# First attention head's loads placed behind the gate blocks, two buffers for the scans' gates, one buffer ring for the scans' level copies

## The chip, the core and the metric

The kernel runs on one core of a Trainium2 chip. The metric is the device time of one execution in microseconds (us). Before the change the median of three runs is 3580.6 us (3577.68 to 3582.16). The engines are named as in the profile: PE is TensorE (PEld its weight loads), DVE is VectorE, ACT is ScalarE, POOL is GpSimd, SP is SyncE, which here only issues DMAs. Each engine takes its instructions in order, and so does each queue of DMA issues.

## What is computed

Two layers of a hybrid encoder on x of 2048 tokens by 1024 features. One input projection of 4128 columns feeds three groups of heads: four heads of gated linear attention and four of HGRN2, both as two-way scans in chunks, and four heads of differential softmax attention. Each group's output is normalised and multiplied by its own SiLU gate; one output projection, a norm and the residual end the layer.

```python
for layer in range(DEPTH):
    h = rms_norm(x, norm_pre[layer])
    proj = h @ w_in[layer]
    (gq, gk, gv, gg, gaf, gab, dq, dk, dv, dg, hq, hzf, hzb, hi, hg) = jnp.split(proj, offs, axis=-1)
    y_a = gla_branch(gq, gk, gv, gg, gaf, gab, ...)      # two scans, forward and backward
    y_b = diff_branch(dq, dk, dv, dg, ...)               # softmax(q1 k1) - lam * softmax(q2 k2), times v
    y_c = hgrn_branch(hq, hzf, hzb, hi, hg, ...)         # two scans
    y = jnp.concatenate([y_a, y_b, y_c], axis=-1) @ w_out[layer]
    x = x + rms_norm(y, norm_post[layer])
```

## The kernel before

**Stages of a layer.** The tokens are cut into two halves ("parts" 0 and 1), the input projection into 18 blocks of columns (lists `first` and `rest`). The loop at the end of the stage `s1` first runs all blocks for part 0, then all for part 1, and during part 1 the scans. Then come attention (`Unit`, with the scans' state products `Inter` between) and the output projection. In layer 0 part 1 with the scans lies at about 405 to 986 us of the span, attention at 986 to 1600 us; in layer 1 at about 2172 to 2765 us and 2765 to 3380 us.

**The blocks of part 1.** Blocks 9 and 10 are the attention values, 11 and 12 its keys, 13 and 14 its queries (`do_qk`), 15 to 17 gates (`do_gate`). A block of part 1 gets its weights `whi`, `wlo` (1 MB each) again from `dr_w` on POOL's DMA queue (line 226, two buffers). A block of `do_qk` makes products in PSUM (line 330), which DVE (lines 369, 371), POOL (372, 375) and ACT (374) turn into `u` and `rh`; both are stored to `dr_q` or `dr_k` by SP (377, 378). A block of `do_gate` makes its products at line 339; DVE copies them to `z` (428), ACT and DVE make the sigmoid in `lsm` (354, 430), POOL multiplies by the norm weight `nw` (432) and by `lsm` (433), SP stores to `dr_gate` (434). `nw` has one buffer and is loaded by SP (412). All these row tiles (`u`, `rz`, `rh`, `z`, `lse`, `lsm`) share one ring of six buffers (`EVB`), and a tile that is stored keeps its buffer until its store has landed. The products of part 1 have four PSUM banks.

**The scans.** There are 12 groups: 3 kinds (`ti`: one of the linear attention, two of HGRN2) for each of 4 stretches of 512 tokens. `scan_group` is a generator of 8 steps; a group starts 5 steps behind the last one (`LAG`), and `SCHED` says how far the scans have been written out behind each block. A group loads `qr`, `kt` and its decay gates `gt` (SP; lines 546 and 550). `gt` has one buffer (`GTB`); it is read by line 560, and as the totals of level 1 by lines 649, 651 and 657. The levels 3 to 7 multiply masked copies of `kt` and `qt`: ACT makes `qp`, `kp` for the linear attention in a ring of six buffers (`QMB`, tag `qm`), `kc`, `qc` for HGRN2 in one of four (`KCB`, tag `kc`), and PE multiplies them (600, 619). `qt` has two buffers and is stored to `dr_qs` by SP (683) at the end. The diagonal goes by PE transposes (671) and DVE sums `dg` (672), products with the values (692) and states (714, stored to `dr_u` at 733) end a group.

**The first head's loads.** When block 14 has been written out, the scans' buffers are given back and the pool `ak` takes their place. `load_q` loads the queries of three pairs of 128-query blocks (24 DMAs of 64 KB on SP, line 774), `head_keys(0)`, behind block 15, the keys (4 DMAs of 512 KB, on POOL's queue for the first head, line 754), `head_values(0)`, behind block 16, the values (1 MB on POOL's queue, line 761).

**What sets the order.** Up to the end of the projection a scheduler decides each engine's order, with a timeline of its own, from the order in which the code is written, the priorities and the buffers. In attention the order is written out by hand.

Of the kernel before, what the change touches and what calls it, by code (L numbers as in the profile page):

```python
# [11 lines left out]
F32 = mybir.dt.float32  # L12
# [9 lines left out]
P = 128  # L22
# [7 lines left out]
KC = D // P  # L30
EVB = 6
EPB = 4
KCB = 4
PRB = 4
ATB = 3
QMB = 6
OIB = 1
QSB = 3
QRB = 1
GTB = 1  # L40
VB = 1
TTB = 1
SCHED = [2, 4, 6, 6, 6, 6, 6, 6, 6, 9, 12, 12, 12, 12, 12, 12, 12, 12]
# [18 lines left out]
def tile_hybrid_encoder(  # L62
# [9 lines left out]
    nc = tc.nc  # L72
# [219 lines left out]
    for l in range(DEPTH):  # L292
# [15 lines left out]
        with ExitStack() as s1:  # L308
# [71 lines left out]
            def t2_rows(ap, t2):  # L380
                return ap[256 * t2:256 * t2 + 256, :].rearrange("(j p) c -> p j c", p=P)
# [19 lines left out]
                        nc.sync.dma_start(dr_vr[t0:t0 + 1024, i].rearrange("(c p) n -> c p n", p=P),  # L401
                                          bass.AP(odd.tensor, odd.offset + (P - 1) * 512, [(P * 512, 8), (-512, P), (1, 64)]))

            low = {}

            def do_gate(c0, d0, part):
                w = wload(c0, 288 if d0 == 0 else 256, part)
                nw = ev.tile([P, 256], F32, tag="nw", name="nw", bufs=1)
                src = {0: gla_norm, 768: hgrn_norm}.get(d0, diff_norm)
                n = src.shape[-1]  # L410
                for i in range(0, 256, n):
                    nc.sync.dma_start(nw[:, i:i + n], src[l:l + 1].to_broadcast([P, n]))
                if src is diff_norm:
                    nc.vector.tensor_scalar(nw, nw, 1.0 - lam_init, None, op0=ALU.mult)
                for t2 in range(4 * part, 4 * part + 4):
                    z = ev.tile([P, 512], F32, tag="t", name="z")
                    if d0 == 0:
                        if t2 % 2 == 0:
                            low[t2 // 2] = ev.tile([P, 4, 32], F32, tag="low", name="low", bufs=2)
                        for j in range(2):  # L420
                            t = 2 * t2 + j
                            ps = acc([P, 288], "pp", part)
                            mm_rows(ps, w, t, 288)
                            nc.vector.tensor_copy(z[:, 256 * j:256 * j + 256], ps[:, :256])
                            nc.scalar.copy(low[t2 // 2][:, t % 4], ps[:, 256:])
                    else:
                        ps = mm_time(w, t2)
                        nc.vector.tensor_copy(z, ps.rearrange("p j c -> p (j c)"))
                    _, m = log_sig(z)
                    nc.scalar.activation(m, m, AF.Exp)  # L430
                    zn = z.rearrange("p (j c) -> p j c", j=2)
                    nc.gpsimd.tensor_tensor(zn, zn, nw.unsqueeze(1).to_broadcast([P, 2, 256]), op=ALU.mult)
                    nc.gpsimd.tensor_tensor(z, z, m, op=ALU.mult)
                    nc.sync.dma_start(t2_rows(dr_gate, t2)[:, :, d0:d0 + 256], zn)

            def do_ch(c0, dst, scale, part):
                w = wload(c0, 256, part)
# [92 lines left out]
            sc = sc_st.enter_context(tc.tile_pool(name=f"sc{l}", bufs=1, side="left"))  # L530

            def scan_group(ti, g, tot):
# [18 lines left out]
                v = sc.tile([P, 4, ncol], F32, tag="v", name="v", bufs=VB)  # L551
# [27 lines left out]
                def gla_level(h, m2):  # L579
                    arr = [(2 * h, m2), (h, 2), (1, h)]  # L580
                    pms = []
                    for b in range(2):
# [4 lines left out]
                        back = [(P, 2), (-2 * h, 64 // h), (-1, h)]  # L587
                        qp = sc.tile([P, 2, 256], F32, tag="qm", name="qp", bufs=QMB)
                        for i in range(2):
# [16 lines left out]
                def hgrn_level(h, n2):  # L606

                    m = n2
                    arr = [(2 * h, m), (h, 2), (1, h)]
                    kc = sc.tile([P, 512], F32, tag="kc", name="kc", bufs=KCB)  # L610
                    nc.scalar.copy(custom(kc, 0, arr), custom(kt, 0, [(2 * h, m), (512 + h, 2), (1, h)]))
                    qc = sc.tile([P, 512], F32, tag="kc", name="qc", bufs=KCB)
                    nc.scalar.copy(custom(qc, 0, arr), custom(qt, 512, [(2 * h, m), (h - 512, 2), (1, h)]))
                    pm = [one_bank([P, 4, P], "pm") for _ in range(2)]
                    for c in range(4):
                        cs = slice(c * P, (c + 1) * P)
                        for hd in range(2):
                            rows = slice(64 * hd, 64 * hd + 64)
                            nc.tensor.matmul(pm[hd][:, c], kc[rows, cs], qc[rows, cs], start=True, stop=True)  # L619
                    return [(atp[0][:, hd], pm[hd], 0) for hd in range(2)]  # L620
# [3 lines left out]
                for lev in range(1, 8):  # L624
                    if lev > 2:
                        yield
                    h = 1 << (lev - 1)
# [119 lines left out]

            kv, qs_of, ga_of = {}, {}, [None]

            def head_keys(h):  # L750
                k = ak.tile([P, 2, L], F32R, tag="ks", name="ks", bufs=2)
                r = slice(64 * (h % 2), 64 * (h % 2) + 64)
                for p0 in range(0, P, 32):
                    (nc.sync if h else nc.gpsimd).dma_start(
                        k[p0:p0 + 32].bitcast(F32), dr_k[h // 2, p0 // 64, p0 // 32 % 2, r].rearrange("(c p) t -> p c t", p=32))
                ks = [k[:, 0], k[:, 1]]
                kv[h] = [ks, None]

            def head_values(h):
                v = ak.tile([P, NT, P], F32, tag="vt", name="vt", bufs=2)  # L760
                nc.gpsimd.dma_start(v, dr_v[:, h * P:(h + 1) * P].rearrange("(c p) n -> p c n", p=P))
                kv[h][1] = v

# [4 lines left out]
            def load_q(h, qp):  # L768
                qh = ak.tile([P, 2, 256], F32R, tag="aqh", name="aqh", bufs=3)
                ql = ak.tile([P, 2, 256], F32R, tag="aql", name="aql", bufs=3)  # L770
                r = slice(64 * (h % 2), 64 * (h % 2) + 64)
                for i, q in enumerate((qh, ql)):
                    for p0 in range(0, P, 32):
                        nc.sync.dma_start(q[p0:p0 + 32].bitcast(F32), dr_q[h // 2, p0 // 64, i, r, qp * 256:(qp + 1) * 256]
                                          .rearrange("(c p) t -> p c t", p=32))
                qs_of[h, qp] = qh, ql
# [8 lines left out]
            for i, b in enumerate(first + rest):  # L785
                b(1)
                scans(LAG * SCHED[i] if i < SC_END else len(work))
                if i == SC_END:
                    sc_st.close()
                    psum_close("m")  # L790
                    psum_open("t", f"pst{l}", "right")
                    at_st = ExitStack()
                    ak = at_st.enter_context(tc.tile_pool(name=f"ak{l}", bufs=1, side="left"))
                    for qp in range(3):
                        load_q(0, qp)
                if i == SC_END + 1:
                    head_keys(0)
                if i == SC_END + 2:
                    head_values(0)
            w_in_st.close()  # L800
            psum_close("s")
            psum_open("b", f"psb{l}", "left")
# [387 lines left out]
```

## Time and profile before

| | |
|---|---|
| median of the runs | 3580.6 us |
| the profiled execution | 3580.0 us, span 3578.0 us |
| PE busy | 3491.2 us, 98% of the span |
| DVE, ACT, POOL busy | 65%, 57%, 36% |
| granted clock of PE, mean | 0.988 |
| DMA | 544.59 MB, mean 152 GB/s |

The profile's busy time of PE counts matmuls whose ends are modelled, so a busy PE is not a PE at its best. Stretches are read by window: the busy time of each engine, the granted clock (1.00 is 2.4 GHz, 0.50 is 1.2 GHz), and the share of time in which the DMA engines were busy.

### The profile page before, as it was taken

To read this page: it belongs to the slowest core of one execution; us is meant where nothing else is said; L and a number is where in the kernel's file an instruction comes from. 1 tells how busy PE (TensorE), PEld (TensorE's weight loads), DVE (VectorE), ACT (ScalarE), POOL (GpSimd) and SP (SyncE) were. 2 spreads that over 40 slices of the span, in tenths; PEclk is the share of its full clock that TensorE was granted. 3 is DMA by queue.
4 is the path that set the end of the run, shared out by engine and by line. 5 is a ranking of instruction groups with operands and counts; after the bars stand their busy time and mean duration, and the time that the engine had idled before them with its cause. 6 is when DMAs were issued, how large, how long until landed. Compare 5 with 4: busy or idle time off the path is not lost.

```text
span 3578.0 us, 62684 instructions
## 1 busy us (share of the span) xinstructions
PE 3491.2 (98%) x23296; PEld 3151.1 (88%) x23296; DVE 2331.3 (65%) x4164; ACT 2046.3 (57%) x4692; POOL 1280.7 (36%) x1302
## 2 busy tenths in 40 slices
PE   7999999999899999999999999999998999999999
PEld 7898988988889999998898999889888889999887
DVE  5333578775299988985324336777843998989733
ACT  4531457653378888874226225576524888888722
POOL 4237310013466655610032472000134765656100
PEclk9999999999999999999999999999999999999999
DMA  6667545545653353214356665555465423433143
GB/s 238 214 230 241 202 151 172 164 145 179 184 140 75 108 137 100 89 50 156 121 205 232 221 228 180 172 163 167 134 190 167 129 73 116 132 93 101 35 135 118
DMA packets 323120, 544.59 MB, mean 152 GB/s; under 512 B 49088, under 2 KB 208512, under 8 KB 304128
## 3 DMA queue, kind: packets, MB, share of 16 engines
q1 hardware_dynamic: 300032, 426.54, 37.8%
q0 software_dynamic: 20672, 111.94, 9.8%
q8 instruction: 185, 3.03, 0.4%
q10 hardware_dynamic: 2112, 2.10, 0.2%
q14 instruction: 119, 0.97, 0.1%
HBM read 313.83 MB, written 228.59 MB: 152 GB/s over the span
## 4 chain that ended last, share of the span: by engine, by line
PE 75%; DVE 13%; DMA 5%; ACT 4%; issue 1%; SPq 1%; POOL 0%; DVEq 0%; ACTq 0%; POOLq 0%
PE pp L339 15%; PE pp L330 15%; PE po L991 10%; PE pob L1100 9%; PE s L928 5%; PE s L929 5%; PE pt L980 5%; DVE mx L933 4%; PE pm L619 2%; DVE e L974 2%; PE po L692 2%; PE pu L714 1%; PE poi L875 1%; DMA dr_q<-rh 1%; DMA gt<-dr_gg 1%
## 5 line engine op out<-in xcount | busy, mean ns | idle before, releaser
L933 DVE TENSOR_REDUCE mx<-s 128x1 f32<-128x1024 f32 x512 | 623.2, 1218 | 59.5 <-PE s L929 58.0
L339 PE MATMUL pp<-whi,hhi 128*128 128x256 f32 (+1 forms) x2048 | 591.5, 289 | 19.9 <-issue 14.2
L942 ACT ACTIVATE e<-s,mx 128x1024 f32<-128x1024 f32 x512 | 572.7, 1123 | 30.1 <-DVE mx L933 12.0
L339 PE MATMUL pp<-wlo,hhi 128*128 128x256 f32 (+1 forms) x2048 | 588.9, 288 | 0.0
L339 PE MATMUL pp<-whi,hlo 128*128 128x256 f32 (+1 forms) x2048 | 587.7, 287 | 0.4 <-DVE hlo L198 0.4
L991 PEld LDWEIGHTS po<-vt,wt 128*128 128x128 f32 x4096 | 534.3, 191 | 46.0 <-ACT o L998 3.5
L991 PE MATMUL po<-vt,wt 128*128 128x128 f32 x4096 | 540.1, 275 | 1.6 <-ACT o L998 1.6
L928 PE MATMUL s<-ks,aqh 128*128 128x512 f32 x1024 | 449.8, 439 | 12.9 <-ACT e L942 11.2
L339 PEld LDWEIGHTS pp<-whi,hhi 128*128 128x128 f32 x2048 | 393.8, 192 | 23.1 <-issue 21.7
L330 PE MATMUL pp<-hhi,whi 128*128 128x512 f32 x1024 | 407.7, 398 | 0.0
L330 PE MATMUL pp<-hlo,whi 128*128 128x512 f32 x1024 | 406.7, 397 | 0.0
L330 PE MATMUL pp<-hhi,wlo 128*128 128x512 f32 x1024 | 404.5, 395 | 0.0
L929 PE MATMUL s<-ks,aql 128*128 128x512 f32 x1024 | 403.4, 394 | 0.0
L339 PEld LDWEIGHTS pp<-whi,hlo 128*128 128x128 f32 x2048 | 394.2, 193 | 1.8 <-DVE hlo L198 0.8
L339 PEld LDWEIGHTS pp<-wlo,hhi 128*128 128x128 f32 x2048 | 393.4, 192 | 1.6 <-issue 0.2
L984 ACT COPY wt<-pt 128x512 f32<-128x512 f32 x512 | 301.3, 588 | 152.3 <-PE pt L980 149.2
L974 DVE SCALAR_TENSOR_TENSOR e<-e,gam 128x1024 f32<-128x1024 f32 x256 | 350.0, 1368 | 0.0
L980 PE MATMUL pt<-ident,e 128*128 128x128 f32 x2048 | 307.8, 273 | 0.4 <-ACT wt L984 0.3
L226 POOL DMA_DIRECT2D whi<-dr_w x32 | 17.6, 550 | 667.5 <-PE pp L339 341.7
L980 PEld LDWEIGHTS pt<-ident,e 128*128 128x128 f32 x2048 | 239.9, 141 | 1.8 <-ACT wt L984 1.0
L928 PEld LDWEIGHTS s<-ks,aqh 128*128 128x128 f32 x1024 | 194.9, 190 | 42.5 <-ACT e L942 18.2
L330 PEld LDWEIGHTS pp<-hhi,whi 128*128 128x128 f32 x1024 | 192.7, 188 | 43.5 <-issue 0.2
(184 smaller groups left out, 6846.2 us busy)
## 6 DMA issues: line engine op xcount, KB each, us to landing
dr_w<-whi SPq DMA_DIRECT2D x30, 1024.0 KB, 3.9
dr_w<-wlo SPq DMA_DIRECT2D x30, 1024.0 KB, 4.9
whi<-dr_w POOLq DMA_DIRECT2D x30, 1024.0 KB, 5.5
wlo<-dr_w POOLq DMA_DIRECT2D x30, 1024.0 KB, 8.6
wraw<-in_w_in_dram POOLq DMA_DIRECT2D x56, 512.0 KB, 6.3
dr_gate<-z SPq DMA_DIRECT2D x64, 256.0 KB, 2.4
aqh<-dr_q SPq DMA_DIRECT2D x256, 64.0 KB, 2.1
aql<-dr_q SPq DMA_DIRECT2D x256, 64.0 KB, 2.1
```

Of the source, the lines that this page charges most:

```text
L330: nc.tensor.matmul(ps.rearrange("p (a t) -> p a t", t=P), w[a][:, k, c:c + P], b[g][:, :, k], start=n == 0, stop=n == 3 * KC - 1)
L339: nc.tensor.matmul(ps, b[g][:, t % 4, k], w[a][:, k, :n], start=cnt == 0, stop=cnt == 3 * KC - 1)
L619: nc.tensor.matmul(pm[hd][:, c], kc[rows, cs], qc[rows, cs], start=True, stop=True)
L928: nc.tensor.matmul(s[:, i], self.qh[:, c, js], kk, start=True, stop=False)
L929: nc.tensor.matmul(s[:, i], self.ql[:, c, js], kk, start=False, stop=True)
L933: nc.vector.tensor_reduce(mx[:, k:k + 1], self.s[k].rearrange("p a n -> p (a n)"), axis=AX.X, op=ALU.max, negate=True)
L942: nc.scalar.activation(self.es[c][:, n * 1024:(n + 1) * 1024], self.s[kk].rearrange("p a n -> p (a n)"), AF.Exp, bias=self.mx[:, m:m + 1], ...
L974: nc.vector.scalar_tensor_tensor(es[0][:, hs], es[1][:, hs], gm[:, 8 + n:9 + n], es[0][:, hs], op0=ALU.mult, op1=ALU.add)
L980: nc.tensor.transpose(pt[:, i], self.es[0][:, (4 * q + i) * P:(4 * q + i + 1) * P], ident)
L984: nc.scalar.copy(wt, self.pt[q])
L991: nc.tensor.matmul(self.po, self.wt[q][:, i], self.v[:, k], start=k == 0, stop=k == NT - 1)
L1100: nc.tensor.matmul(pos[:, n], a[:, k], b[k][:, n * 512:(n + 1) * 512], start=cnt == 0, stop=cnt == 3 * KC - 1)
```

## The change

It does three things. `GTB` goes from 1 to 2. `kc` and `qc` leave their ring of four and share the ring `qm` with `qp` and `kp`, which grows from six to eight buffers. And the first head's loads are made to wait: `do_gate` keeps its last `lsm` in `late[0]`; `after_block` has DVE copy one column of it into the tile that is about to be loaded, so that the load, which writes the same tile, stands behind that copy. The keys of head 0 so stand behind the last sigmoid of block 15, the values and the first three pairs of queries behind that of block 16; the queries are also written out later, behind block 16. It adds 8 copies of one column to DVE in each layer and takes nothing away.

```diff
-KCB = 4
-QMB = 6
+QMB = 8
-GTB = 1
+GTB = 2
...
                     nc.gpsimd.tensor_tensor(z, z, m, op=ALU.mult)
                     nc.sync.dma_start(t2_rows(dr_gate, t2)[:, :, d0:d0 + 256], zn)
+                    late[0] = m
...
-                    kc = sc.tile([P, 512], F32, tag="kc", name="kc", bufs=KCB)
+                    kc = sc.tile([P, 512], F32, tag="qm", name="kc", bufs=QMB)
...
-                    qc = sc.tile([P, 512], F32, tag="kc", name="qc", bufs=KCB)
+                    qc = sc.tile([P, 512], F32, tag="qm", name="qc", bufs=QMB)
...
+            def after_block(t):
+                nc.vector.tensor_copy(t, late[0][:, :1])
             def head_keys(h):
                 k = ak.tile([P, 2, L], F32R, tag="ks", name="ks", bufs=2)
+                if not h:
+                    after_block(k[:, 0, :1])
...
                 v = ak.tile([P, NT, P], F32, tag="vt", name="vt", bufs=2)
+                if not h:
+                    after_block(v[:, 0, :1])
...
                 for i, q in enumerate((qh, ql)):
+                    if not h and qp < 3:
+                        after_block(q[:, 0, :1])
...
-                    for qp in range(3):
-                        load_q(0, qp)
                 if i == SC_END + 1:
                     head_keys(0)
                 if i == SC_END + 2:
                     head_values(0)
+                    for qp in range(3):
+                        load_q(0, qp)
```

The scheduler moves many instructions with it. Line numbers of the changed program differ from those before by -1 (from line 40 on) up to +10 (from line 809 on).

SP's queue of DMA issues at the end of block 14, layer 0, before the change: `aqh`, `aql` are the first head's queries, `dr_q` the stores of the query blocks, `dr_u` the last states of the scans.

```order
L377 DMA dr_q<-rh 128x512 x2
L378 DMA dr_q<-ru 128x512 x2
L696 DMA dr_oi<-oi 128x4x128
L733 DMA dr_u<-ut 64x3x128
L733 DMA dr_u<-ut 64x4x128
L774 DMA aqh<-dr_q 32x2x256 x4
L774 DMA aql<-dr_q 32x2x256 x3
L377 DMA dr_q<-rh 128x512
L774 DMA aql<-dr_q 32x2x256
```

The same queue after the change, from the last states of the scans to the last gate block (`ks` are here the second head's keys).

```order
L733 DMA dr_u<-ut 64x4x128
L790 DMA aga<-dr_gate 128x2x128 x3
L376 DMA dr_k<-rh 128x512
...
L760 DMA ks<-dr_k 32x2x2048 x2
L433 DMA dr_gate<-z 128x2x256 x4
L784 DMA aqh<-dr_q 32x2x256 x4
L784 DMA aql<-dr_q 32x2x256 x3
L433 DMA dr_gate<-z 128x2x256
...
L784 DMA aql<-dr_q 32x2x256 x4
L411 DMA nw<-in_hgrn_norm_dram 128x64 x4
L850 DMA woraw<-in_w_out_dram 128x1024 x2
```

The 24 query loads have moved from between the stores of the query block to behind those of the gate block 16, ahead of the load of `nw` for block 17. The scans' last stores have moved from block 14 up into block 12. On PE 106 projection matmuls (line 330) stood between the last product of a scan and the first of a gate block; now 271 do, in both layers.

POOL at the end of block 14, layer 0, before the change: weights of block 15, then the first head's keys and values.

```order
L226 DMA whi<-dr_w 128x2048
L226 DMA wlo<-dr_w 128x2048
L372 TENSOR_TENSOR ru<-ru,rz 128x512
L754 DMA ks<-dr_k 32x2x2048 x4
L761 DMA vt<-dr_v 128x16x128
L375 TENSOR_TENSOR ru<-ru,rh 128x512
```

POOL after the change, from the weights of block 17 on.

```order
L225 DMA whi<-dr_w 128x2048
L225 DMA wlo<-dr_w 128x2048
L431 TENSOR_TENSOR z<-z,nw 128x512
L760 DMA ks<-dr_k 32x2x2048 x4
L432 TENSOR_TENSOR z<-z,lsm 128x512
...
L769 DMA vt<-dr_v 128x16x128
L432 TENSOR_TENSOR z<-z,lsm 128x512
```

The keys have moved from behind the weights of block 15 to behind those of block 17, the values four multiplications of block 16 further.

SP where a group of the scans begins, layer 0, before the change: `gt<-dr_gg` are the gates of a group of the linear attention, `dr_qs` is the end of the group before it.

```order
L733 DMA dr_u<-ut 64x2x256 x2
L543 DMA qr<-dr_qkg 128x512
L546 DMA gt<-dr_gg 128x2x512
L683 DMA dr_qs<-qt 64x2x512 x2
L396 DMA dr_v<-vs 128x2x256
```

The same load after the change.

```order
L733 DMA dr_u<-ut 64x4x128 x2
L683 DMA dr_qs<-qt 64x2x512 x2
L548 DMA qr<-dr_qh 128x512
L546 DMA gt<-dr_gg 128x2x512
L395 DMA dr_vs<-vs 128x2x256 x2
```

It has moved up by one group: it now follows the load of `qr` of the group before its own.

## Rows read from the trace of the kernel before

**Rows 1.** The chain of work that ended last, some of its longest pieces over the whole span: start, us, what and how often.

```profile
76.69 22.38 PE pp L330 x96
...
718.28 8.79 DMA gt<-dr_gg
...
888.39 20.99 DMA dr_q<-rh
916.51 8.24 DMA dr_q<-ru
928.35 57.84 PE pp L339 x480
...
2665.73 19.74 DMA dr_q<-rh
```

**Rows 2.** Timeline of PE in four places, two in each layer: start, us, operation, in brackets the idle time before it and what ended that.

```profile
912.41 0.55 PE L339 MATMUL pp<-whi,hhi 128*128 128x256 f32 x1 [7.77 <-issue]
...
928.35 0.36 PE L339 MATMUL pp<-whi,hhi 128*128 128x256 f32 x1 [2.07 <-DVE ru L369]
...
2688.51 0.55 PE L339 MATMUL pp<-whi,hhi 128*128 128x256 f32 x1 [6.38 <-issue]
...
2705.51 0.35 PE L339 MATMUL pp<-whi,hhi 128*128 128x256 f32 x1 [3.65 <-DVE ru L369]
```

**Rows 3.** DMA issues by line: count, KB each, median us from issue to landing.

```profile
aqh<-dr_q SPq DMA_DIRECT2D x256, 64.0 KB, 2.1
...
dr_q<-rh SPq DMA_DIRECT2D x32, 256.0 KB, 4.6
...
vt<-dr_v POOLq DMA_DIRECT2D x8, 1024.0 KB, 9.0
```

**Rows 4.** Timelines of SP's queue (two rows) and of POOL (four rows) at the end of block 14 of layer 0.

```profile
884.83 2.01 SPq L774 DMA_DIRECT2D aqh<-dr_q  x4
...
888.39 0.42 SPq L377 DMA_DIRECT2D dr_q<-rh  x1
...
882.96 0.55 POOL L226 DMA_DIRECT2D whi<-dr_w  x1 [10.35 <-PE pp L330]
...
885.29 2.18 POOL L754 DMA_DIRECT2D ks<-dr_k  x4
887.46 1.19 POOL L761 DMA_DIRECT2D vt<-dr_v  x1
...
910.33 1.26 POOL L372 TENSOR_TENSOR ru<-ru,rz 128x512 f32<-128x512 f32 x1 [17.10 <-DVE rz L371]
```

**Rows 5.** Busy time by window: the window, its length, busy us (instructions) of PE, PEld, DVE, ACT and POOL, the granted clock of PE, the share of time in which the DMA engines were busy, GB/s. Four stages of layer 0, then short windows around stops of PE: four of layer 0, two of layer 1.

```profile
500.00:600.00 100.00, 97.65 (x614) 83.65 (x613) 77.54 (x144) 69.19 (x156) 3.21 (x6) 1.00 0.53 172
600.00:700.00 100.00, 97.55 (x774) 91.83 (x773) 81.58 (x160) 72.32 (x167) 2.10 (x4) 0.97 0.53 171
...
888.00:928.00 40.00, 30.50 (x170) 27.14 (x168) 4.55 (x7) 2.35 (x4) 11.92 (x11) 0.87 0.92 253
928.00:986.00 58.00, 57.66 (x480) 57.69 (x481) 16.31 (x25) 29.59 (x46) 32.65 (x27) 1.00 0.45 144
...
910.00:920.00 10.00, 7.58 (x46) 7.62 (x47) 1.63 (x3) 0.62 (x1) 4.88 (x5) 0.64 0.79 258
...
930.00:940.00 10.00, 10.00 (x86) 10.00 (x85) 1.38 (x2) 1.26 (x3) 2.58 (x2) 1.00 0.98 287
...
729.50:739.70 10.20, 9.98 (x48) 9.09 (x49) 8.78 (x16) 3.29 (x7) 0.00 (x0) 0.50 0.09 27
739.70:750.00 10.30, 10.30 (x89) 9.54 (x89) 5.43 (x12) 2.24 (x5) 0.00 (x0) 1.00 0.47 130
...
2507.50:2518.00 10.50, 10.40 (x51) 9.50 (x52) 8.67 (x16) 3.48 (x7) 0.00 (x0) 0.52 0.09 27
...
2684.00:2694.00 10.00, 5.49 (x32) 5.52 (x33) 2.08 (x3) 1.24 (x2) 5.57 (x6) 0.66 0.67 184
```

**Rows 6.** Timelines of DVE and PE where a group of the scans begins, in both layers.

```profile
727.17 0.69 DVE L657 TENSOR_TENSOR nt<-gt 128x512 f32<-128x512 f32 x1 [4.86 <-DMA gt<-dr_gg]
...
2505.05 0.69 DVE L657 TENSOR_TENSOR nt<-gt 128x512 f32<-128x512 f32 x1 [5.66 <-DMA gt<-dr_gg]
...
729.72 0.48 PE L692 MATMUL po<-v,att 128*128 128x64 f32 x1 [4.24 <-DVE dg L672]
...
2507.60 0.32 PE L692 MATMUL po<-v,att 128*128 128x64 f32 x1 [4.50 <-DVE dg L672]
```

**Rows 7.** The last gate block and the start of attention in layer 0: timelines of SP's queue, POOL and DVE.

```profile
970.24 1.30 SPq L412 DMA_DIRECT2D nw<-in_hgrn_norm_dram  x3
...
978.57 1.29 POOL L432 TENSOR_TENSOR z<-z,nw 128x512 f32<-128x512 f32 x1 [6.98 <-DVE lsm L354]
...
977.84 0.69 DVE L354 SCALAR_TENSOR_TENSOR lsm<-z,lse 128x512 f32<-128x512 f32 x1 [2.40 <-DMA dr_gate<-z]
...
987.13 2.35 DVE L933 TENSOR_REDUCE mx<-s 128x1 f32<-128x1024 f32 x2 [0.22 <-PE s L929]
```

**Rows 8.** Other stops of PE where groups of the scans begin, layer 0: timeline of PE.

```profile
582.67 0.33 PE L671 MATMUL pd<-ident,pr 128*128 128x128 f32 x1 [1.32 <-DVE dg L672]
...
657.15 0.32 PE L675 MATMUL pdr<-dg,flip 128*128 128x64 f32 x1 [2.39 <-DVE dg L672]
```

**Rows 9.** Who waited for whom, DVE between 405 and 882 us: us in total, times, longest.

```profile
DVE qt L560 <- DMA dr_qs<-qt: 11.8, 4, 5.7
```

More of the change, by code (lines that the diff above doesn't have):

```diff
@@ L402, in do_vs @@
                                           bass.AP(odd.tensor, odd.offset + (P - 1) * 512, [(P * 512, 8), (-512, P), (1, 64)]))
-            low = {}
+            low, late = {}, [None]
             def do_gate(c0, d0, part):
```

## The prediction

> **What bounds the kernel now.** The page's table of busy time says that PE is busy for 98% of the span, so a change can gain only where PE stops or runs at the lower clock. I therefore read the chain of waits first, then PE's timeline at its gaps, then the windows around them. The chain's longest pieces that are not matmuls [rows 1] are one store in each layer, `dr_q<-rh`, of 20.99 and 19.74 us, where the median of its kind is 4.6 [rows 3], and the load of `gt` at 718 us, 8.79 us. Around these, and only around these, PE stops for more than 3 us between the begin of the scans and attention.
>
> *First place, the end of block 14.* Between 883 and 889 us POOL issues the weights of block 15, four loads of keys and one of values, and SP the first queries, just ahead of the store [rows 4]. The DMA engines are then busy for 0.92 of 888 to 928 us at 253 GB/s, and for 0.45 of the 58 us after it [rows 5]. The store holds a buffer of the ring of six, POOL sits 17.10 us behind DVE's next step [rows 4], the PSUM banks fill, and PE stops for 7.77 and 2.07 us in layer 0, for 6.38 and 3.65 us in layer 1 [rows 2].
>
> *Second place, a group of the linear attention.* Its `gt` can be fetched only when the group before has read the single buffer. DVE waits 4.86 and 5.66 us for it, and PE behind DVE's sums 4.24 and 4.50 us [rows 6].
>
> After each stop the granted clock drops from 1.00 (2.4 GHz) to 0.50 (1.2 GHz) for some us [rows 5].
>
> **What the change does, part by part.**
>
> *Holding the loads back* takes 4 x 512 KB of keys, 1 MB of values and 24 x 64 KB of queries, 4.7 MB, out of the stretch in which the store waits: 18.6 us of DMA at 253 GB/s. The stores of block 14 then meet the traffic of blocks 11 to 13, which have the same weights and stores and no such stop. I count all four stops of [rows 2]: 9.84 us and 10.03 us. Then the clock: in 910 to 920 us 46 matmuls take 7.58 us where 86 take 10.00 at full clock, 0.116 us each [rows 5]; 46 x 0.116 = 5.3, so 2.2 us are lost. In layer 1, 32 in 5.49 us: 1.8 us. Sum of the first term: **-23.9 us**, bounds -23.9 and 0.
>
> *The second `gt` buffer* lets the load go one group earlier, as SP's order shows. The stops of 4.24 and 4.50 us go. The lower clock behind them costs 9.98 - 48 x 0.116 = 4.4 us in layer 0 and 10.40 - 51 x 0.116 = 4.5 us in layer 1 [rows 5]. Sum of the second term: **-17.6 us**. What is late next there is `qt`: DVE already waits 11.8 us in four places until `qt` has been stored [rows 9].
>
> *The hand-over to attention.* The loads must now arrive under the gate blocks. By the chain, 480 matmuls of the gate blocks take 57.84 us [rows 1], so a block of 192 takes 23.1 us and the three 69 us. Keys may go when block 15 has been evicted, 46 us before the end: 2 MB is 8.3 us at 253 GB/s. The second head's keys, another 2 MB, stand beside them, and still it is 17 us. Queries and values may go when block 16 is through, 23 us before the end; SP needs 2.01 us for four issues [rows 4], so 12 us for 24, and the last lands 2.1 us later [rows 3]; the values take 9.0 us and are wanted later still. So the loads themselves fit and cost nothing, with some 9 us to spare for the queries; if that cover is gone, their wait is the start of attention.
>
> What does not fit as well is queued behind them. The load of `nw` for block 17 now stands behind the 24 query loads on SP. Before, it was issued at 970.24 us with nothing ahead of it, and POOL's first multiplication with it came 8.3 us later [rows 7]. Now it is up to 12 us later, while block 17's products come as fast as ever. With six buffers only two sub-blocks of gates are in flight (DVE's `lsm` already waits 2.40 us for a store [rows 7]); the third's copy waits for the first's store, and DVE's first maximum of attention stands behind that copy, where before it came at 987.13 us with 0.22 us of idle time [rows 7]. Four PSUM banks hide it from the gate blocks' matmuls, not from attention. The same goes for block 16's stores and `nw`, which share SP with the second head's keys. Bounds 0 and 12 us per layer; I take half, 6. Third term: **+12 us**.
>
> The 8 copies of one column cost DVE well under 0.69 us each, the row of a copy-sized operation [rows 6], beside a DVE that is busy for 16.31 of 58 us there [rows 5]: nothing. POOL's weights of block 17 now stand behind three sub-blocks of block 15, but they wait for PE to leave block 15 anyway: nothing.
>
> *The denser scans.* 271 instead of 106 projection matmuls follow the scans, so the scheduler packs the scans by 165 matmuls of 0.233 us (22.38 us for 96 [rows 1]), 38 us of some 476 (405 to 881 us). DVE, busy for 78 to 82% there [rows 5], goes to 84 to 89%. The trace has no scans so dense. From below: the shared ring of eight lets ACT run further ahead, and the stops of 1.32 and 2.39 us [rows 8] with one stretch of low clock (4.4 us) may go, -8 us per layer. From above: each group start may stop PE as at 657 us. I take one more stop of about 3 us per layer, nearest to the rows of today: **+6 us**.
>
> **Sum.** 3580.0 us (the profiled execution; its span is 3578.0) - 23.9 - 17.6 + 12 + 6 = 3556.5; the median stands 0.6 above that execution, so **3557 us**.
>
> **The rivals.**
>
> *The hand-over eats the first gain.* All 12 us of SP's issues appear at the start of attention in each layer: 12 more, 3569 us. For it: the order on SP, and the six buffers. Against: the four banks, and that SP may get its queries out while block 17 runs. Chance 0.16.
>
> *The loads come late.* The bulk of the first head's loads is not hidden at all: 18.6 us per layer instead of 6, 25 more, 3582 us, no change. The trace speaks against it: 0.45 of the DMA time is used in the gate blocks, and 144 of 253 GB/s [rows 5]. Chance 0.04. On this point the Trainium skill's page "DMA: Bandwidth & Descriptors", section "Rules for kernel authors", advises to issue a DMA early and to wait on its semaphore late, which speaks for the kernel before; the trace differs, since there the early loads cost a store 20.99 us.
>
> *The denser scans stop PE (slower).* In the scans PE stands behind DVE's sums at each of 24 group starts. One stop as at 657 us with the low clock behind it is 2.39 + 4.4 = 6.8 us. Without the 6 us taken, 29.5 us are gained, so from five more such stops on nothing is left; with eight it is 3580.6 - 29.5 + 54 = 3605 us. For it: DVE at up to 89%, and `dr_qs` stores placed later on SP, on which `qt` waits. Against: of 12 starts in layer 0 only a few stop PE now, and DVE's waits include long ones for PE itself. Chance 0.08.
>
> *The second buffer does nothing.* `qt`, not `gt`, holds the group: the second term is lost, 3574.6, say 3575 us, within 0.2%. Against: both waits name `gt` alone [rows 6]. Chance 0.10.
>
> *No new cost at all.* The third and fourth terms are 0 and -16: 3580.6 - 41.5 - 16 = 3523 us. Chance 0.06.
>
> The forecast keeps 0.56, with 3545 to 3568 us as its own range.
>
> **How the numbers follow.** About 0.2% (7 us) is what a measurement of this kernel can tell from no change. Faster by more than that are the forecast, the first rival and the last, 0.78, and a little of the lost buffer: 0.79. Within 0.2% is the rest of that and the late loads: 0.13. Slower is the rival of the scans: 0.08. The range must take in the first rival and the lost buffer at the upper end; at the lower end the hand-over at its bound of 0 and the scans at -8 per layer for half: 3535 to 3577 us. It leaves out most of the slower rival and of the cheapest case.
>
> **What would show it.** Right: `dr_q` stores of block 14 land in about 5 us, PE goes from block 14 into block 15 without a gap or a drop of the clock, and DVE's waits for `gt` are gone. In the third term: `nw` of the last block issued after the queries, a late first maximum, and PE waiting at its first scores. The fourth is right if PE's gaps in the scans, apart from the two of [rows 6], stay about as many. The forecast is wrong if PE stops behind `dg` at many group starts, if the gates' stores grow as long as `dr_q`'s were, or if the first scores wait for keys or queries.

## The result, and the profile after

The changed kernel takes 3628.9 us in the median (3621.6 to 3638.3), the kernel before 3579.1 us beside it: ratio 1.0139, 95% interval 1.0114 to 1.0165. The forecast was 3557 us, 0.6% faster; it is 1.4% slower, and outside the range. The profiled execution of the changed kernel took 3621.6 us, its span is 3619.7 us, 41.7 us more than before.

The table divides each layer at four points of PE's timeline: the first transpose of a scan, the last product of block 14, the last product of the gate blocks, and the first product of the output projection.

| us | layer 0 before | after | layer 1 before | after | both | predicted |
|---|---|---|---|---|---|---|
| scans, to the end of block 14 | 479.4 | 494.6 | 488.0 | 494.1 | +21.3 | -11.6 |
| from there to the end of the gates | 81.6 | 69.3 | 82.8 | 69.3 | -25.8 | -23.9 |
| from there to the output projection | 613.7 | 639.2 | 615.5 | 635.8 | +45.8 | +12 |
| sum | | | | | +41.3 | -23.5 |

"Predicted" puts the second and the fourth term into the first row. One row came as forecast, two missed by 33 and 34 us.

**The end of block 14.** DMA issues by line, of the kernel after, issued between 870 and 930 us, the two of layer 0's query block: count, KB each, median us from issue to landing.

```profile
dr_q<-rh SPq DMA_DIRECT2D x8, 256.0 KB, 2.5
dr_q<-ru SPq DMA_DIRECT2D x8, 256.0 KB, 2.1
```

Two landings of each kind are recorded; they took 2.5 and 2.1 us in the median, where one took 20.99 us before [rows 1]. PE goes into the gate blocks in both layers without idle time, at 919.47 and 2716.88 us below, where it had stood for 7.77 and 6.38 us [rows 2].

**The hand-over.** Timelines of four engines of the kernel after, in order of time, layer 0 from 919 us, and at the end layer 1: start, us, operation, in brackets the idle time before it and what ended that.

```profile
919.47 0.28 PE L338 MATMUL pp<-whi,hhi 128*128 128x256 f32 x1
...
943.74 0.94 SPq L760 DMA_DIRECT2D ks<-dr_k  x2
...
947.99 2.21 POOL L760 DMA_DIRECT2D ks<-dr_k  x4
...
948.07 0.84 SPq L411 DMA_DIRECT2D nw<-in_diff_norm_dram  x2
...
969.33 0.29 DVE L413 TENSOR_SCALAR nw<-nw 128x256 f32<-128x256 f32 x1 [11.48 <-DMA nw<-in_diff_norm_dram]
...
969.75 2.55 POOL L431 TENSOR_TENSOR z<-z,nw 128x512 f32<-128x512 f32 x2 [18.23 <-DVE nw L413]
...
981.89 0.14 DVE L752 CAST aqh<-lsm 128x1 fp32r<-128x1 f32 x1
...
982.07 2.69 SPq L784 DMA_DIRECT2D aqh<-dr_q  x4
...
992.62 0.76 PE L938 MATMUL s<-ks,aqh 128*128 128x512 f32 x1 [3.87 <-DMA aqh<-dr_q]
...
998.29 1.85 SPq L411 DMA_DIRECT2D nw<-in_hgrn_norm_dram  x4
...
1007.58 2.48 POOL L431 TENSOR_TENSOR z<-z,nw 128x512 f32<-128x512 f32 x2 [22.61 <-DMA nw<-in_hgrn_norm_dram]
...
1011.31 1.73 DVE L353 SCALAR_TENSOR_TENSOR lsm<-z,lse 128x512 f32<-128x512 f32 x1 [15.19 <-POOL z L432]
...
1013.08 0.69 DVE L427 COPY z<-pp 128x512 f32<-128x512 f32 x1
...
1013.92 0.77 PE L938 MATMUL s<-ks,aqh 128*128 128x512 f32 x1 [19.06 <-DVE z L427]
...
2716.88 0.28 PE L338 MATMUL pp<-whi,hhi 128*128 128x256 f32 x1
...
2808.04 0.77 PE L938 MATMUL s<-ks,aqh 128*128 128x512 f32 x1 [21.89 <-DVE z L427]
```

Read it upwards from 1013.92. The second pair of scores needs a PSUM bank that still holds products of block 17. DVE's copy `z<-pp` would free it, but it stands on DVE behind `lsm`, which needs one of the six row buffers, which POOL holds until `nw` of block 17 is there. That `nw` was issued at 998.29, behind the 24 queries, 28 us later than before [rows 7], and POOL had it 9 us after that. And the queries went only at 982.07, since their one-column copies waited for block 16's sigmoid, and block 16 had its own `nw` late: issued at 948.07 as two loads of 64 KB, between keys of two heads, it kept DVE waiting until 969.33, 21 us, and DVE and POOL stood idle meanwhile. In layer 1 it is the first pair of scores that waits for such a bank, 21.89 us.

Busy time by window, of the kernel after; the columns are those of [rows 5].

```profile
993.00:1023.00 30.00, 8.98 (x20) 6.00 (x20) 8.89 (x11) 8.51 (x14) 10.01 (x8) 0.50 0.31 104
...
919.50:988.50 69.00, 69.00 (x577) 69.00 (x575) 15.72 (x31) 26.76 (x41) 31.20 (x29) 1.00 0.71 184
940.00:972.00 32.00, 32.00 (x269) 32.00 (x268) 5.76 (x10) 8.49 (x13) 10.65 (x12) 1.00 0.88 196
```

The gate blocks run at full clock without a gap, and the DMA engines are busy for 0.88 of the 32 us in which block 16's `nw` is under way. Then PE works for 9 of 30 us at the clock of 1.2 GHz.

**The scans.** Timeline of PE in the kernel after, layer 0: three of the new stops, and three rows of level products.

```profile
482.41 2.05 PE L619 MATMUL pm<-qc,kc 64*128 64x128 f32 x24
...
489.40 2.07 PE L619 MATMUL pm<-qc,kc 64*128 64x128 f32 x8 [4.05 <-DVE ut L718]
...
495.41 2.38 PE L619 MATMUL pm<-qc,kc 64*128 64x128 f32 x32
...
520.56 2.60 PE L619 MATMUL pm<-qc,kc 64*128 64x128 f32 x32
...
609.34 1.63 PE L619 MATMUL pm<-qc,kc 64*128 64x128 f32 x10 [4.05 <-DVE att L645]
...
658.35 1.94 PE L671 MATMUL pd<-ident,pr 128*128 128x128 f32 x8 [5.30 <-DVE pr L577]
```

The stops behind `gt` [rows 6] are gone in both layers, those of [rows 8] in layer 0; others stand in their place. Groups of PE's instructions between the first transpose of a scan and the first score, layer 0, kernel after (424.6 to 992.6 us): busy us, mean ns, idle time before and what ended it.

```profile
L619 PE MATMUL pm<-qc,kc 64*128 64x128 f32 x640 | 68.5, 300 | 13.8 <-DVE att L645 8.9 <-DVE ut L718 4.1 <-DVE dg L672 0.7
...
L671 PE MATMUL pd<-ident,pr 128*128 128x128 f32 x192 | 28.5, 288 | 7.9 <-DVE pr L577 5.8 <-ACT att L641 1.7 <-DVE dg L672 0.4
```

The same view of the kernel before (424.9 to 986 us), the row that answers to the first of these and was not read for the prediction.

```profile
L619 PE MATMUL pm<-qc,kc 64*128 64x128 f32 x640 | 63.9, 290 | 0.0
```

The same row in layer 1, the kernel before (2193.7 to 2765.5 us) and after (2222.5 to 2808 us).

```profile
L619 PE MATMUL pm<-qc,kc 64*128 64x128 f32 x640 | 67.5, 302 | 0.0
...
L619 PE MATMUL pm<-qc,kc 64*128 64x128 f32 x640 | 66.7, 297 | 8.6 <-DVE ut L718 3.9 <-DVE att L645 2.5 <-ACT ktt L707 1.4
```

In layer 0 the HGRN2 levels' products (640 records) cost PE 4.6 us more, in layer 1 0.8 us less. What is common to both layers is the idle time before them, 13.8 and 8.6 us where there was none: several levels lie back to back and wait for DVE, in layer 0 mostly until it has taken levels ahead of them out of PSUM (`att`, 8.9 us).

### The profile page after: what moved, and what is told of

It is laid out like the page before. It is cut to its first block, busy times and chain, and to the rows that moved or that the text cites. A ratio compares the mean times of both kernels' runs of the same rounds, so it can differ in the third digit from the quotient of the medians.

```text
span 3619.7 us, 62634 instructions
## 1 busy us (share of the span) xinstructions
PE 3490.5 (96%) x23296; PEld 3150.3 (87%) x23296; DVE 2335.2 (65%) x4180; ACT 2038.8 (56%) x4692; POOL 1268.9 (35%) x1302
## 5 line engine op out<-in xcount | busy, mean ns | idle before, releaser
L329 PEld LDWEIGHTS pp<-hhi,wlo 128*128 128x128 f32 x1024 | 195.0, 190 | 45.6 <-issue 1.1
```

The source lines that it names most:

```text
L329: nc.tensor.matmul(ps.rearrange("p (a t) -> p a t", t=P), w[a][:, k, c:c + P], b[g][:, :, k], start=n == 0, stop=n == 3 * KC - 1)
```

## The experiments

Two theories came from this. **N**: the hand-over is lost to the one tile of norm weights. **R**: the scans are lost to the shared ring of copies, through the order that the scheduler makes of it. Their rivals stand in the expectations. The ratios are to the kernel before measured beside each run (3583.0 to 3586.7 us), so runs are compared by ratio. The last two columns divide each profiled execution as the table above does, with its first two rows taken together: us against the kernel before, both layers added. For the whole change they are -4.5 and +45.8.

| run | what it is | us | ratio to before, 95% interval | to the end of the gates | from there on |
|---|---|---|---|---|---|
| e1 | loads held back, nothing else | 3608.5 | 1.0068 (1.0046 to 1.0090) | -27 | +46 |
| e2 | ring of eight and two gate buffers | 3604.6 | 1.0057 (1.0042 to 1.0072) | +21 | -1 |
| e3 | ring of eight alone | 3608.6 | 1.0069 (1.0054 to 1.0084) | +30 | -2 |
| e4 | e1 with norm weights apart | 3560.2 | 0.9923 (0.9905 to 0.9940) | -32 | +15 |
| e5 | e1 with the second head's keys held | 3591.9 | 1.0021 (1.0005 to 1.0037) | -27 | +30 |
| e6 | before with norm weights apart | 3574.2 | 0.9968 (0.9955 to 0.9982) | -4 | -2 |
| e7 | two gate buffers, two for the copies | 3555.1 | 0.9908 (0.9890 to 0.9925) | -45 | +21 |
| e8 | the whole change with norm weights apart | 3581.9 | 0.9989 (0.9974 to 1.0004) | -15 | +16 |
| e9 | two buffers for the copies alone | 3558.2 | 0.9916 (0.9887 to 0.9945) | -45 | +23 |
| e10 | e4 and e7 | 3539.4 | 0.9861 (0.9838 to 0.9883) | -54 | +14 |
| e11 | e6 and e7 | 3540.4 | 0.9860 (0.9834 to 0.9885) | -57 | +15 |
| e12 | shared ring of four | 3573.5 | 0.9966 (0.9952 to 0.9980) | -9 | 0 |
| e13 | six for the copies, four for `qm`, apart | 3607.1 | 1.0058 (1.0039 to 1.0076) | +29 | -3 |
| e14 | e6 and e9 | 3549.1 | 0.9897 (0.9881 to 0.9914) | -48 | +14 |

**e1, e2, e3: the change in parts.** e1 has the diff's lines on `late`, `after_block` and `load_q` only; e2 and e3 these, e3 without the last:

```diff
-KCB = 4
-QMB = 6
+QMB = 8
-                    kc = sc.tile([P, 512], F32, tag="kc", name="kc", bufs=KCB)
+                    kc = sc.tile([P, 512], F32, tag="qm", name="kc", bufs=QMB)
...
-GTB = 1
+GTB = 2
```

> Only the first head's loads are held back; one gt buffer and the two old rings stay. Theory H (the hand-over to attention costs more than the freed store gains: the load of nw for block 16 lands late behind the second head's keys, the queries and the nw of block 17 follow late): block 14 runs into block 15 without a stop (about -12 us per layer), PE stops some 20 us before the second or third scores of attention in each layer; in all 3579 - 24 + 45 = about 3600 us, slower by 0.3 to 0.8%. Rival S (all of the loss comes from the denser scans): 3555 us, faster, and no stop above 5 us at the start of attention.

> Only the buffers: two for gt, one ring of eight for the level copies; the loads as before the change. Theory H with its second part (the denser scans cost some 10 us per layer by stops at DVE's pr, att and ut, more than the two waits for gt gave): 3579 + 20 = about 3600 us. Rival S: 3620 us or more. Rival B (buffers gain the 18 us that the waits for gt cost, the loss is all the hand-over's): 3562 us.

> Only the shared ring of eight for the level copies; one gt buffer, loads as before. If the second gt buffer is what packs the scans, this is 3575 to 3585 us with the waits for gt still there. If the shared ring is what packs or stops them, it is as slow as the run with both buffers changed, about 3600 us.

e1 and e2 came out slower, as theory H had it. The two halves add up: 1.0068 x 1.0057 is 1.0125, the whole change 1.0139 with an interval that holds it. They add up by place too: up to the end of the gates -27 and +21 us against -4.5, from there on +46 and -1 against +45.8. e1 has the gates' 69 us and the hand-over's loss together: its last row would be 636.2 and 639.5 us. (The gates take 69 us in e2 and e3 as well, but there the early loads only stop PE sooner, ahead of the gates, in e3 by 7.70 us at 922.83; so the first two rows are read together.) e3 shows that the ring alone costs as much as both edits of buffers together.

What the buffers do to the scans is cleanest between e1 and the whole change, which hold the loads alike. Busy time by window, from the first transpose to the last gate product, e1 and the kernel after in layer 0, then both in layer 1; the columns are those of [rows 5].

```profile
424.00:976.20 552.20, 539.59 (x3830) 488.88 (x3828) 369.52 (x695) 299.94 (x686) 95.84 (x89) 0.98 0.53 166
...
424.60:988.80 564.20, 542.41 (x3830) 493.10 (x3828) 367.01 (x690) 291.79 (x671) 91.16 (x89) 0.97 0.51 162
...
2206.80:2759.90 553.10, 541.41 (x3830) 491.13 (x3829) 370.03 (x695) 299.31 (x684) 95.83 (x89) 0.98 0.53 165
...
2222.50:2786.20 563.70, 541.72 (x3830) 492.24 (x3828) 371.20 (x694) 295.75 (x683) 91.16 (x89) 0.97 0.52 163
```

Of the 22.6 us that the buffers cost here, 3.1 are more busy time of PE and 19.5 are more idle time.

**e4, e6: norm weights in tiles of their own.** Loaded once per layer, in part 0 (in e4 at 26.6 to 29.9 us of the span), so that no block of part 1 loads any:

```diff
-                nw = ev.tile([P, 256], F32, tag="nw", name="nw", bufs=1)
...
-                for i in range(0, 256, n):
-                    nc.sync.dma_start(nw[:, i:i + n], src[l:l + 1].to_broadcast([P, n]))
+                key = min(d0, 256) + d0 // 768
+                if key not in norm_of:
+                    norm_of[key] = ev.tile([P, n], F32, tag=f"nw{key}", name="nw", bufs=1)
+                    nc.sync.dma_start(norm_of[key], src[l:l + 1].to_broadcast([P, n]))
...
+                nw = norm_of[key]
...
-                    nc.gpsimd.tensor_tensor(zn, zn, nw.unsqueeze(1).to_broadcast([P, 2, 256]), op=ALU.mult)
+                    z3 = z.rearrange("p (j c) -> p j c", c=n)
+                    nc.gpsimd.tensor_tensor(z3, z3, nw.unsqueeze(1).to_broadcast([P, 512 // n, n]), op=ALU.mult)
```

> Loads held back as in e1, and each of the three norm weights in a tile of its own (64, 128 and 64 columns in place of one of 256), loaded once per layer, so that blocks 15 to 17 load none of them. Theory N (the hand-over of e1 is lost to the norm weights' tile: block 17's weights land behind queries and keys, its GpSimd product, VectorE's copies and the first scores' banks wait): the stop of about 20 us before the second pair of scores goes, at most 5 us of it is left per layer; e1's gates of 69 us stay; 3560 us, 0.6% faster than before. Rival B (the held loads themselves are late, queries or keys, whatever the norm weights do): the stop stays within 5 us of e1's and the time within 3600 to 3612 us.

> The kernel before with the three tiles of norm weights and nothing else: a control for e4. Theory N and both rivals: there the norm weights were on time but for a wait of about 1 us, so no difference, 3575 to 3587 us. If it is over 0.3% faster, e4's gain is not the hand-over's.

Who waited for whom, e1: us in total, times, longest.

```profile
PE s L939 <- DVE z L428: 44.4, 2, 25.2
```

The same of e4.

```profile
PE s L942 <- DVE z L430: 6.0, 2, 3.7
```

38 us of PE's wait for DVE's copies are gone, and the time falls by 1.4%, to 3560 us as theory N gave it. With the norm weights out of the way the held loads pay. e6, expected at no difference, is 0.3% faster, just at the limit that its expectation set for doubting e4. The last two columns settle it: of the 36 us that e4's profiled execution gains on e1's, 31 lie behind the gates, where the stop was; e6 gains 2 us there. What e6 gains by itself was not found, and it is a fifth of what e4 gains on e1.

Theory N is not the whole hand-over, though: behind the gates e4 still takes 15 us more than the kernel before, 7 and 8 per layer. Timelines of SP, ACT and PE in e4, layer 0.

```profile
980.14 0.89 SPq L437 DMA_DIRECT2D dr_gate<-z  x2
...
982.64 0.63 ACT L350 ACTIVATE lse<-z 128x512 f32<-128x512 f32 x1 [3.89 <-DMA dr_gate<-z]
...
987.26 0.79 PE L942 MATMUL s<-ks,aqh 128*128 128x512 f32 x1 [6.41 <-ACT e L956]
```

POOL had done the two rows of gates by 973.9, but their stores were issued only at 980.14, behind the last queries on SP. ACT's `lse` waits until one of them has landed and given its buffer back, and the next scores wait for what ACT does after it. This is read from the rows; no run tests it.

**e5: the second head's keys behind block 16.**

```diff
-                        head_load(f // 64 + 1)
+                        head_load(f // 64 + 1, units[1].gm[:, 8:9] if f == 16 else None)
```

> Loads held back as in e1, and the second head's keys wait for block 16's gate as well, so that the norm weights of block 16 do not stand behind them on SyncE's queue. Theory N: block 16's norm weights land within 10 us of their issue in place of 21, but block 17's still stand behind the 24 query loads; half of the hand-over's loss goes, 3590 us, and a stop of about 10 us is left before the second pair of scores. Rival S (SyncE's order does not matter, the DMA engines are simply full with the held loads): block 16's norm weights still take over 15 us and the time stays at 3600 to 3612 us.

Timelines of SP and DVE in e5, layer 0.

```profile
940.23 0.85 SPq L412 DMA_DIRECT2D nw<-in_diff_norm_dram  x2
...
955.58 0.29 DVE L414 TENSOR_SCALAR nw<-nw 128x256 f32<-128x256 f32 x1 [11.05 <-DMA nw<-in_diff_norm_dram]
...
982.63 1.85 SPq L412 DMA_DIRECT2D nw<-in_hgrn_norm_dram  x4
```

The time is as expected, the place less so: block 16's `nw` still takes 15 us beside the first head's keys, not under 10, which was the rival's sign; block 17's still stands behind the queries, and PE still stops for 16.1 and 14.0 us at the scores, not for about 10. Clearing one of the two queues ahead of `nw` gives back about a third of what e4 does.

**e8: the whole change, norm weights apart.** The edit of e4 on the changed kernel.

> The whole change, and the three norm weights in tiles of their own as in e4. Theory N + R (two costs that add: the norm weights' tile at the hand-over, and the shared ring in the scans): the hand-over's stop goes as from e1 to e4, by 1.4%, and the ring's cost stays: 3575 to 3585 us, no faster than the kernel before. Rival (the two costs are one, in that the ring's order makes the norm weights late or hides in their wait): either 3560 us or less, or above 3600 us.

It gives back 1.5% and ends where the kernel before is. The two costs add; what is left against e4, 0.66%, is what the buffers cost.

**e7, e9: fewer buffers for the copies.** e9 is the first line pair, e7 both:

```diff
-KCB = 4
+KCB = 2
-GTB = 1
+GTB = 2
```

> The kernel before with two buffers for the scans' gates, paid for with two in place of four buffers for the level copies kc and qc, in a ring of their own, so that the ring shared with qm is not there. Theory R (the shared ring alone lengthens the scans, by letting the scheduler set levels back to back; the second gate buffer gains): the stops on gt go, the scans are 5 to 9 us shorter per layer, 3565 us. Rival G (the second gate buffer packs the scans by itself, whatever ring the copies have; or two buffers stop the copies): the scans are 10 us or more longer per layer, 3600 us or more.

> The kernel before with two buffers in place of four for the level copies, and one gate buffer as before: a control for e7. Theory R: the second gate buffer gives most of e7's gain, so this one stays within 0.4% of before, 3570 to 3595 us, with the stops on gt still there. Rival K (a tight ring for the copies keeps the levels apart, and by that alone gives e7's gain): 3560 us or less.

e7 is faster, as theory R had it, by more than it said (3555 us, not 3565), and for another reason: e9 shows that the two buffers for the copies bring nearly all of it. Theory R's second part, that the second gate buffer gains, falls here, and rival K holds. Timeline of PE in e9, layer 0, the same stretch as above.

```profile
475.55 1.16 PE L619 MATMUL pm<-qc,kc 64*128 64x128 f32 x8
...
488.59 1.16 PE L619 MATMUL pm<-qc,kc 64*128 64x128 f32 x16
...
495.57 1.16 PE L619 MATMUL pm<-qc,kc 64*128 64x128 f32 x16
...
881.34 0.28 PE L339 MATMUL pp<-whi,hhi 128*128 128x256 f32 x1
...
978.43 0.80 PE L928 MATMUL s<-ks,aqh 128*128 128x512 f32 x1 [9.58 <-DVE z L428]
```

Groups of PE's instructions in e9 (424.4 to 967.8 us), the level products.

```profile
L619 PE MATMUL pm<-qc,kc 64*128 64x128 f32 x640 | 53.6, 290 | 0.0
```

With two buffers a level cannot start before the level ahead of it has been multiplied, so each level stands by itself among projection products: sixteen records in 1.16 us, and 53.6 us for all of layer 0 where the kernel before needs 63.9 and the changed one 68.5. The scans also end later, behind the first gate products, so that the first queries are issued at 928.81 us, 36 us behind the last issue of a query block's store for its `ru` (892.87): the order holds the loads back by itself, and PE enters the gate blocks at 881.34 without a gap. From the first transpose to the first score layer 0 takes 543.4 us instead of 561.1. Part of this is lost again: the scores after the first ones wait 9.58 us for DVE's copy of block 17's products, and from the end of the gates on e9 takes 23 us more than the kernel before in both layers.

Who waited for whom in e9.

```profile
PE po L692 <- DVE dg L672: 1.1, 2, 0.5
...
DVE nt L657 <- DMA gt<-dr_gg: 8.5, 4, 3.8
```

DVE waits for `gt` still, but PE no longer stands behind it.

**e10, e11, e14: the gains together.** e10 is e4 with the lines of e7, e11 the same without the held loads, e14 is e11 with `GTB = 1`.

> Loads held back with the norm weights in tiles of their own (e4), and two gate buffers with two for the level copies (e7). Theory N + R (two gains in two places): the ratios multiply to 0.983, 3523 us. Rival O (e7 has no stop between blocks 14 and 15 any more, so both gain the same stop): 3545 to 3560 us.

> e6 and e7 together, with the first head's loads where the kernel before has them: what e10 has without the holding back. Theory N + R: e7's stop of about 9 us on the way to the second pair of scores goes, 3540 us, and e10 is faster by the held loads. Rival O: as fast as e10 or faster, 3535 to 3550 us, since holding the loads back gains nothing once the order has changed.

> e11 with one gate buffer. Theory D: e9 and e7 stand within 0.1% of each other, so the second gate buffer is worth nothing here either: within 0.2% of e11's 0.986, 3533 to 3540 us. Rival (the second gate buffer's 17.6 us of the prediction come back once nothing else holds TensorE): 3550 us or more.

e10 and e11 take the same time, 1.4% less than the kernel before: in this order holding the loads back gains nothing (rival O), though e10 came nearer to the product of both gains than that rival had it. e14 is 0.37% slower than e11, more than theory D allowed and 1 us short of the 3550 us of the rival. By the pairs e3 and e2, e9 and e7, e14 and e11 the second gate buffer is worth 0.12, 0.08 and 0.37%, 4, 3 and 13 us, with intervals that overlap each time.

**e12, e13: sharing or size.** e12 is e3 with `QMB = 4`; e13:

```diff
-KCB = 4
+KCB = 6
-QMB = 6
+QMB = 4
```

> The kernel before with its level copies in one ring with qm, as in e3, but of four buffers in place of eight. In its order 0.24 of the copies' 640 products stand in rows of twelve or more (before 0.19, e3 0.55, e9 0.00). Theory D (what decides is how many copies fit ahead of TensorE, by the order that the scheduler makes of it): within 0.4% of before, 3570 to 3598 us. Rival Sh (sharing a ring is what costs, whatever its size): 0.5% slower or more, 3600 us.

> The kernel before with six in place of four buffers for the level copies and four in place of six for qm, each in its own ring; 0.29 of the products stand in rows of twelve or more. Theory D: looser than before, so slower, by 0.2 to 0.6%, 3590 to 3605 us, and not as slow as e3. Rival Sh: no shared ring, so as before, 3575 to 3590 us.

Groups of PE's instructions in e13 (424.3 to 1001.7 us).

```profile
L619 PE MATMUL pm<-qc,kc 64*128 64x128 f32 x640 | 67.7, 291 | 0.0
```

A small shared ring costs nothing, a large one of the copies' own does: sharing is not the cause, and theory D holds as far as these runs go. (e13 also has two buffers fewer for `qm`; e12 has four for `qm` and the copies together and loses nothing by it. Whether e13 is less slow than e3, as was expected, can't be told: the intervals overlap.) The more copies may run ahead, the slower the kernel was: rings of 2, 4 shared, 4, 6 and 8 shared give 0.9916, 0.9966, 1, 1.0058 and 1.0069. By what step is shown only in part. The share of products in rows of twelve or more (nothing else between them in PE's order) is no law: e12 has a larger one than before and is a little faster, and e6 has 0.45 and is faster too. And in e13 PE stands idle before none of the level products and spends 3.8 us more on them in layer 0, while scans and gates together take 15 us longer there. Which rows of an order cost how much stays open.

## Why the prediction was wrong

**The first term was right**: -23.9 us forecast, -25.8 measured, and e1, which holds the loads back and does nothing else, gains 27 us up to the end of the gates. The stores land in time and PE crosses into the gate blocks at full clock.

**The third term is the first of three steps that failed**, and it was mis-sized. The prediction named the mechanism: `nw` of block 17 behind the queries on SP, six buffers, the PSUM banks, the first maximum. Its bound, "0 and 12 us per layer; I take half, 6", holds only the issuing of 24 loads. Measured are 25.5 and 20.3 us per layer. In layer 0 `nw` of block 17 was issued 28 us later than before (970.24 [rows 7], now 998.29). Of these, 16.2 us are the issues ahead of it (982.07 to 998.29), not 12, and 11.8 us are the queries' own lateness (970.24 to 982.07). The latter comes from "block 16's stores and `nw`", which the prediction named without a price: that `nw` was 21 us on its way. From its issue to POOL's product block 17's took 9.3 us, before 8.3, so its landing adds next to nothing. e4 and e8 show this cause by taking it away: some 30 of the 46 us go, and what is left is near the 12 us that were forecast. The claim that the loads "cost nothing, with some 9 us to spare" also failed by 3.87 us in layer 0, where the first score waits for queries that had been put off.

The trace of the kernel before had a warning. The 12 us came from four issues in 2.01 us [rows 4], but further down the same queue four took 8.50 us, since SP there waited for earlier loads to land:

```profile
896.03 8.50 SPq L774 DMA_DIRECT2D aqh<-dr_q  x4
```

**The fourth term is the second.** It counted +3 us per layer, with DVE's load as the mechanism and the larger ring as a likely gain ("the shared ring of eight lets ACT run further ahead, and the stops ... may go"). The scans did get shorter, in layer 0 by 22 us in place of 38 (455.7 to 433.5 us from the first transpose to the last state product), but DVE was busy for 0.78 of them after and 0.76 before, not for 0.84 to 0.89. The larger ring cost 0.7% by itself (e3), some 25 us. The scheduler set levels back to back, and PE stood idle before them, 13.8 and 8.6 us; between e1 and the whole change 19.5 of 22.6 us are idle time. The rival that was nearest, "the denser scans stop PE", had the right sign and the right engine, since PE does wait for DVE; but it waits for `att` and `ut` before the level products and for `pr` at the starts of groups, not for the sums `dg` that the rival priced.

The rival "the hand-over eats the first gain" had the same 12 us per layer as its price, and so was about half the size too. The eight copies cost 0.14 us each, which is nothing, as forecast.

**The second term is the third step**: its waits went and its gain did not come. The stops on `gt` are gone, but by the pairs above the buffer is worth 3 to 13 us, not 17.6. That a stop that ends in a tight order is partly given back at the next wait would explain it, but no run shows that.

**On the rule about early loads** the prediction named the Trainium skill's page "DMA: Bandwidth & Descriptors", section "Rules for kernel authors" (issue early, wait late), and set the trace of the kernel before against it. For the bulk loads the trace was right against the rule in the kernel's own order (e4, with the loads held, is faster than e6, without), and it makes no difference in a better order (e10 and e11 are equal). For the small ones the rule is borne out: the norm weights, loaded once and long before their use, gave back 1.4%.

## What to carry to other kernels

Before a bulk load is moved behind a late step, list every small load that will then be issued behind it or beside it, and price each by its issue, the issues ahead of it and its landing under that traffic; a tile of 128 KB with one buffer stopped three engines here. A bigger ring of buffers changes the order of the instructions wherever a scheduler sets it: compare the orders first, and try the smaller ring as well as the larger. When a term of a sum is a bound on one resource, ask what else lies between that resource and the engine that waits.

## What was not expected of the hardware

Level products use 64 of PE's 128 rows, those of one head the lower and those of the other the upper half; each product leaves two records. In e9's rows above the eight records at 475.55 us are the products of one head, by the program's order and the PSUM tiles that it names, and the sixteen at 488.59 us alternate between two heads: both took 1.16 us. By the records' starts in the whole span, the second of a pair begins 5 to 7 ns behind the first, and then about 105 ns pass; in a row that does not alternate each takes about 112 ns. Of neighbours among these products 565 of 1184 start within 20 ns of each other in e9, 389 of 1182 in the kernel before and 353 of 1192 in the changed one. So two products on different halves run side by side, and where an order separates them the same products take about twice as long. Priced at 105 ns for each such neighbour, an estimate from these starts, e9's 176 more are worth 18 us and the 36 fewer of the changed kernel cost 4. Measured over both layers, the level products take 23.4 us less in e9 (in layer 1 54.4 us, before 67.5) and 3.8 us more in the changed kernel. By this estimate most of the difference in their busy time is how the order pairs them.

Two loads of 64 KB (norm weights) kept DVE waiting until 21 us after their issue, beside 4 MB of keys and the weights of a block, while the DMA engines were busy for 0.88 of the time.
